# Interleaving xbc_proj with s5_mixer and rg_mixer, and re-staging four modulation vectors, in a two-block fp32 network

## The chip, the core and the metric

The kernel runs on one core of a Trainium2 chip: TensorE (PE; its weight loads are listed as PEld), VectorE (DVE), ScalarE (ACT), GpSimd (POOL) and SyncE (SP), which here only issues DMAs, each with its own in-order instruction stream, over one SBUF and one PSUM. The metric is device microseconds of one execution. A run's time is a little longer than the span of its trace, which goes from the first to the last instruction.

## What is computed

Two blocks in a row on 1024 tokens of width 1024, in float32. The first is a retention and gated-linear-attention mixer with an MLP, modulated by six vectors from a conditioning vector c. The second is a mixer of three parts (SSD, S5, RG-LRU), then cross attention, then an MLP. The lines that matter here:

```python
mod = jax.nn.silu(c) @ w_ada[l] + b_ada[l]
shift1, scale1, gate1, shift2, scale2, gate2 = jnp.split(mod, 6, axis=-1)
u = _layer_norm(x) * (1.0 + scale1[:, None, :]) + shift1[:, None, :]
...
proj = jnp.einsum('bld,dk->blk', h, w_in[l].astype(f32))
z, xbc, dt_raw, u_s5, x_rg, g_rg = jnp.split(proj, split_idx, axis=-1)
xbc = jax.nn.silu(causal_dwconv(xbc, conv_w.astype(jnp.float32), conv_b.astype(jnp.float32)))
y_s5 = s5_mixer(u_s5, ...)      # diagonal complex scan, gelu, gated linear unit
y_rg = rglru_mixer(x_rg, g_rg, ...)   # conv, two gates, real scan, times gelu(gate)
y = jnp.concatenate([y_ssd, y_s5, y_rg], axis=-1)
```

## The kernel before

Every large product is made of three passes over a high and a low half of its operands (mm3, lines 114 to 116). A weight page is loaded into a staging page of tag S, cast on ACT (L82) and its remainder made on DVE (L83); wcols does this for 256 columns, two staging pages and four pages of tag W. feat_out makes one 128 x 512 result from 24 matmuls into a PSUM bank of tag mm, of which there are two. SBUF is handed out in pages by tag, and the counts set how far work can run ahead: X 8, H 8, W 8, S 6, bc 3.

The order on each engine is not written by hand. The Tile framework takes the program's order as priority and plans every engine's order ahead of time, with its own estimates of durations: an instruction whose inputs and pages are there goes ahead of an earlier one that waits. On the chip each engine then keeps that order, whether or not the estimates were right. A generator's yield is a place where build can put another generator's instructions in between, so it moves priorities only.

Two places matter.

**The later modulation vectors.** scale1 and shift1 are made first (mod_first). The four others, of the order scale2, shift2, gate1, gate2, come from mods: mod_acc adds eight scaled row blocks of w_ada (512 KB each, loaded at L243, added on DVE at L245 and L247) into an accumulator page. mod_feat then takes it through 16 listed matmuls with a column of ones (L259), mod_row through L275, followed by an add and a store. Accumulator and row blocks are all pages of tag bc. mods and then s5_setup are the side generator early(), woven into gla_proj with 0.6 side steps for each of its 26 steps. gla_block, which is woven into the following ret_proj, takes its work pages E and qt from X.

**The input projections of the second mixer.** build calls dt_proj, s5_mixer, xbc_proj and rg_mixer one after the other. s5_mixer holds eight pages of X until its second matrix stage (L1625, L1628) and its gelu. xbc_proj makes eight pages of 128 channels (j = 0 to 7, weights c = j // 2) with two feat_outs each, evicted by ACT to two pages raw and o (L1193, L1194), convolved on DVE (L1176), passed through Tanh (L1197) and a product (L1198) and stored (L1199); raw and o are X pages. rg_mixer makes two feat_outs for each of two halves (L1316, L1317), gates (L1329 to L1334), a chain of Ln, Exp and Sqrt (L1338 to L1343) and a scan (L1345), then two gelu gates (L1351 to L1354) whose weights are Wg. ssd_setup, the loads of the output weights (wout_load, eight staging pages, L659) and the SSD blocks woven with block2_out come behind.

Of the kernel before, what the change touches and what calls it, by code (L numbers as in the profile page):

```python
# [14 lines left out]
S = 1024  # L15
# [9 lines left out]
class Net:  # L25
# [211 lines left out]
    def mod_acc(self, j):  # L237

        nc = self.nc
        acc = self.page("bc")  # L240
        for k in range(8):
            w = self.page("bc")
            nc.sync.dma_start(out=w, in_=self.I["w_ada"][k * 128:(k + 1) * 128, j * 1024:(j + 1) * 1024])  # L243
            if k == 0:
                nc.vector.tensor_scalar(out=acc, in0=w, scalar1=self.silu_c[:, 0:1], scalar2=None, op0=ALU.mult)  # L245
            else:
                nc.vector.scalar_tensor_tensor(out=acc, in0=w, scalar=self.silu_c[:, k:k + 1], in1=acc, op0=ALU.mult,  # L247
                                               op1=ALU.add)
            if k % 4 == 3:
                yield  # L250
        return acc

    def mod_feat(self, j, name, plus=0.0):

        nc = self.nc
        acc = yield from self.mod_acc(j)
        ps = self.ps("tr")
        for k in range(8):
            nc.tensor.matmul(out=ps[:, k:k + 1], lhsT=acc[:, k * 128:(k + 1) * 128], rhs=self.ones[:, 0:1],  # L259
                             start=True, stop=True)  # L260
        m = self.cp.tile([128, 8], F32, name=name)
        nc.vector.scalar_tensor_tensor(out=m, in0=ps[:, 0:8], scalar=plus, in1=self.pvec("b_ada")[:, 8 * j:8 * j + 8],
                                       op0=ALU.add, op1=ALU.add)
        self.mod[name] = m

    def mod_row(self, j, name):

        nc = self.nc
        acc = yield from self.mod_acc(j)
        g = self.small([128, 1024], tag="bc", bufs=self.BUFS["bc"])  # L270
        nc.sync.dma_start(out=g[0:1, :], in_=self.I["b_ada"][0:1, j * 1024:(j + 1) * 1024])
        for h in range(2):
            ps = self.ps()
            sl = slice(512 * h, 512 * h + 512)
            nc.tensor.matmul(out=ps[0:1, :], lhsT=self.ones[:, 0:1], rhs=acc[:, sl], start=True, stop=True)  # L275
            nc.vector.tensor_tensor(out=g[0:1, sl], in0=ps[0:1, :], in1=g[0:1, sl], op=ALU.add)
        d = self.dram([1, 1024], name)
        nc.sync.dma_start(out=d, in_=g[0:1, :])
        self.mod[name] = d

    def mods(self):
        yield from self.mod_feat(4, "scale2", 1.0)
        yield from self.mod_feat(3, "shift2")
        yield from self.mod_row(2, "gate1")
        yield from self.mod_row(5, "gate2")

    def normalize4(self, ys):

# [773 lines left out]
class Mix2(Mix1):  # L1062
# [116 lines left out]
    def xbc_proj(self, T):  # L1179
# [5 lines left out]
        for c in range(4):  # L1185
            W = self.wcols(I["w_in_2"], 512 + 256 * c, 256)
            for m in range(2):
                j = 2 * c + m
                raw, o = self.page("X"), self.page("X")
                for h in range(2):  # L1190
                    sl = slice(512 * h, 512 * h + 512)
                    ps = self.feat_out(T, W, slice(128 * m, 128 * m + 128), h)
# [4 lines left out]
                nc.scalar.activation(out=raw, in_=o, func=ACTF.Tanh)  # L1197
                nc.vector.scalar_tensor_tensor(out=o, in0=raw, scalar=1.0, in1=o, op0=ALU.add, op1=ALU.mult)  # L1198
                nc.sync.dma_start(out=self.s_xd[:, j, :], in_=o)  # L1199

    def ssd_setup(self):
        self.s_St = self.half()
# [88 lines left out]
    def rg_mixer(self, T):  # L1291
        nc, I = self.nc, self.I
        w = I["w_in_2"]
# [17 lines left out]
        for m in range(2):  # L1311
            raw, xc = self.page("X"), self.page("X")
# [5 lines left out]
                                     bias=cb[:, m:m + 1])  # L1318
            self.conv(xc, raw, cw[:, 4 * m:4 * m + 4])
            xcs.append(xc)  # L1320
        Wg = self.wcols(w, 2056, 256)
        ms = []
        for m in range(2):
# [10 lines left out]
            nc.scalar.activation(out=t, in_=r, func=ACTF.Tanh, scale=sm[:, 2 + m:3 + m])  # L1334
            nc.vector.scalar_tensor_tensor(out=gx, in0=gx, scalar=1.0, in1=xc, op0=ALU.add, op1=ALU.mult)
            ms.append((xc, r, gx, t))
        for m, (xc, r, gx, t) in enumerate(ms):
            nc.scalar.activation(out=xc, in_=t, func=ACTF.Ln, bias=1.0)  # L1338
            nc.scalar.activation(out=xc, in_=xc, func=ACTF.Exp, scale=-1.0)
# [2 lines left out]
        for m, (xc, r, gx, t) in enumerate(ms):  # L1342
            nc.scalar.activation(out=t, in_=t, func=ACTF.Sqrt, scale=0.5)  # L1343
            nc.vector.tensor_tensor(out=gx, in0=gx, in1=t, op=ALU.mult)
            nc.vector.tensor_tensor_scan(out=t, data0=r, data1=gx, initial=0.0, op0=ALU.mult, op1=ALU.add)  # L1345
        for m, (xc, r, gx, t) in enumerate(ms):
            x, q = self.page("X"), self.page("X")
            for h in range(2):
# [199 lines left out]
    def s5_mixer(self, T):  # L1548
# [54 lines left out]
        a = [v3(x)[:, :, i0] for x in (Are, Aim)]  # L1603
        p = [v3(x)[:, :, i0] for x in (co, sn)]
        self.cmul(v3(H[0])[:, :, i1], v3(H[1])[:, :, i1], a, p, v3(t)[:, :, i1])
        M = [self.page("H") for _ in range(2)]
        for m in range(2):
            for s in range(8):
# [9 lines left out]
        for m in range(2):  # L1618
# [28 lines left out]
                nc.scalar.activation(out=q[:, sl], in_=ps, func=ACTF.Square)  # L1647
            self.gelu(x, q, x)
            Y.append(x)
        gw = self.half([128, 2, 256])  # L1650
        nc.sync.dma_start(out=gw, in_=I["s5_glu_w_2"].rearrange("(k p) e -> p k e", p=128))
        gb = self.small([128, 8], tag="s5t", bufs=20)
# [130 lines left out]
def build(tc, I, out):  # L1783
    from contextlib import ExitStack
    with ExitStack() as ctx:
# [22 lines left out]
            T = next(norm)  # L1808
        run(kv)
        def early():  # L1810
            yield from n.mods()
            yield from n.s5_setup()
        run(n.weave(n.gla_proj(T), early(), 0.6))
        n.gla_setup()
        run(n.weave(n.ret_proj(T), n.pipe(n.gla_block(i) for i in range(NB)), 0.3))
        n.ret_setup()
# [3 lines left out]
        T = run(n.block1_out())  # L1820
        T = n.block1_mlp(T)
        n.dt_proj(T)
        n.s5_mixer(T)
        n.xbc_proj(T)
        n.rg_mixer(T)
        n.ssd_setup()
        n.wout = n.wout_load(I["w_out_2"])
        out = n.block2_out()
# [90 lines left out]
```

## Time and profile before

| | us |
|---|---|
| median of 3 runs (2730.89 to 2739.81) | 2733.69 |
| the profiled execution, its own time | 2723.2 |
| its span | 2721.4 |
| PE busy | 2572.5 (95%) |
| DVE busy | 1908.2 (70%) |
| ACT busy | 1113.8 (41%) |
| POOL busy | 265.8 (10%) |
| mean granted PE clock, as a share of full speed | 0.964 |

The profiled execution is 10.5 us below the median, and 1.8 us of its time lie outside the span. PE's busy share counts overlapped matmuls; the time between two matmuls of a dense run is what a stretch of PE work takes. A granted clock of 1.00 is the level of 2.4 GHz, 0.50 that of 1.2 GHz, and what lies between is a stretch that had some of both.

### The profile page before, as it was taken

To read this page: it belongs to the slowest core of one execution; us is meant where nothing else is said; L and a number is where in the kernel's file an instruction comes from. 1 tells how busy PE (TensorE), PEld (TensorE's weight loads), DVE (VectorE), ACT (ScalarE), POOL (GpSimd) and SP (SyncE) were. 2 spreads that over 40 slices of the span, in tenths; PEclk is the share of its full clock that TensorE was granted. 3 is DMA by queue.
4 is the path that set the end of the run, shared out by engine and by line. 5 is a ranking of instruction groups with operands and counts; after the bars stand their busy time and mean duration, and the time that the engine had idled before them with its cause. 6 is when DMAs were issued, how large, how long until landed. Compare 5 with 4: busy or idle time off the path is not lost.

```text
span 2721.4 us, 32892 instructions
## 1 busy us (share of the span) xinstructions
PE 2572.5 (95%) x12086; PEld 2085.6 (77%) x12086; DVE 1908.2 (70%) x3237; ACT 1113.8 (41%) x1669; POOL 265.8 (10%) x238
## 2 busy tenths in 40 slices
PE   7898999889999999999999997999997999999997
PEld 7576777677888888888876765778876888888885
DVE  5847765788897777555954558785566877767759
ACT  3522233224654444433642462452236444444332
POOL 4112135540000000000000004200000000000000
PEclk8899999999999999999997998999998999999998
DMA  9674423454266669857641313371101756699774
GB/s 332 210 232 142 147 98 102 142 150 147 78 224 217 214 234 324 287 177 240 202 153 47 110 62 105 111 242 40 54 21 73 246 195 224 230 325 333 271 234 145
DMA packets 255130, 484.36 MB, mean 178 GB/s; under 512 B 21604, under 2 KB 110964, under 8 KB 254968
## 3 DMA queue, kind: packets, MB, share of 16 engines
q1 hardware_dynamic: 247768, 470.59, 51.3%
q10 hardware_dynamic: 7200, 11.67, 1.2%
q8 instruction: 95, 1.56, 0.2%
q14 instruction: 67, 0.55, 0.1%
HBM read 338.80 MB, written 143.38 MB: 177 GB/s over the span
## 4 chain that ended last, share of the span: by engine, by line
PE 76%; DVE 10%; DMA 4%; ACT 4%; issue 3%; POOL 2%; SPq 0%; ACTq 0%; DVEq 0%; POOLq 0%
PE ps L114 23%; PE ps L116 23%; PE ps L115 23%; ACT half L186 1%; PE ps L182 1%; DMA H<-r_qk 1%; DVE half L543 1%; POOL X L522 1%; DMA H<-g_qkb 1%; DMA bc<-in_w_ada 1%; DVE st L155 1%; PE ps L1628 1%; DVE W L83 1%; PE ps L535 1%; POOL W L83 0%
## 5 line engine op out<-in xcount | busy, mean ns | idle before, releaser
L114 PE MATMUL ps<-U,W 128*128 128x512 f32 (+1 forms) x1080 | 426.2, 395 | 11.4 <-ACT X L1352 5.9
L83 DVE TENSOR_TENSOR W<-S,W 128x1024 fp32r<-128x1024 f32 (+1 forms) x272 | 332.8, 1225 | 147.9 <-ACT W L82 145.9
L114 PE MATMUL ps<-W,H 128*128 128x512 f32 x1088 | 425.1, 391 | 3.6 <-DVE sm L167 3.0
L115 PE MATMUL ps<-U,W 128*128 128x512 f32 (+1 forms) x1080 | 424.1, 393 | 0.1
L115 PE MATMUL ps<-W,H 128*128 128x512 f32 x1088 | 424.0, 390 | 0.0
L116 PE MATMUL ps<-W,H 128*128 128x512 f32 x1088 | 423.9, 390 | 0.0
L116 PE MATMUL ps<-U,W 128*128 128x512 f32 (+1 forms) x1080 | 423.5, 392 | 0.0
L82 ACT CAST W<-S 128x1024 fp32r<-128x1024 f32 x288 | 299.2, 1043 | 282.0 <-PE ps L115 200.0
L83 DVE TENSOR_TENSOR H<-S,H 128x1024 fp32r<-128x1024 f32 x130 | 158.8, 1222 | 149.3 <-ACT H L82 138.5
L82 ACT CAST H<-S 128x1024 fp32r<-128x1024 f32 x130 | 136.5, 1050 | 288.6 <-PE ps L115 211.9
L114 PEld LDWEIGHTS ps<-U,W 128*128 128x128 f32 (+1 forms) x1080 | 201.1, 186 | 59.9 <-ACT X L1352 6.3
L114 PEld LDWEIGHTS ps<-W,H 128*128 128x128 f32 x1088 | 204.6, 188 | 47.7 <-DVE X L1014 3.7
L115 PEld LDWEIGHTS ps<-U,W 128*128 128x128 f32 (+1 forms) x1080 | 201.1, 186 | 47.0 <-DVE U L336 2.5
L116 PEld LDWEIGHTS ps<-W,H 128*128 128x128 f32 x1088 | 204.4, 188 | 42.2 <-DVE H L83 0.2
L115 PEld LDWEIGHTS ps<-W,H 128*128 128x128 f32 x1088 | 204.6, 188 | 41.9
L116 PEld LDWEIGHTS ps<-U,W 128*128 128x128 f32 (+1 forms) x1080 | 200.7, 186 | 45.0 <-issue 0.7
L114 PE MATMUL ps<-W,U 128*128 128x512 f32 x352 | 142.0, 403 | 0.0
L115 PE MATMUL ps<-W,U 128*128 128x512 f32 x352 | 140.6, 399 | 0.2 <-DVE W L83 0.2
L116 PE MATMUL ps<-W,U 128*128 128x512 f32 x352 | 140.4, 399 | 0.1
L767 ACT ACTIVATE ev<-ev 128x512 f32<-128x512 f32 x104 | 65.5, 630 | 138.8 <-DVE ev L865 117.3
L1239 POOL TENSOR_TENSOR half<-tri,s_adt 128x512 f32<-128x512 f32 x16 | 19.6, 1233 | 884.5 <-DVE half L1116 778.2
L768 ACT ACTIVATE X<-ev 128x512 f32<-128x512 f32 x128 | 81.1, 636 | 3.5
(527 smaller groups left out, 4606.5 us busy)
## 6 DMA issues: line engine op xcount, KB each, us to landing
S<-mlp_h SPq DMA_DIRECT2D x112, 512.0 KB, 4.8
S<-in_w_ff SPq DMA_DIRECT2D x96, 512.0 KB, 5.1
mlp_h<-X SPq DMA_DIRECT2D x96, 512.0 KB, 3.9
S<-in_mlp_w SPq DMA_DIRECT2D x96, 512.0 KB, 5.2
mlp_w<-S SPq DMA_DIRECT2D x96, 256.0 KB, 2.8
S<-mlp_w SPq DMA_DIRECT2D x48, 512.0 KB, 4.8
S<-in_w_in SPq DMA_DIRECT2D x46, 512.0 KB, 5.2
bc<-in_w_ada SPq DMA_DIRECT2D x32, 512.0 KB, 5.0
```

Of the source, the lines that this page charges most:

```text
L82: self.nc.scalar.copy(out=hi, in_=src)
L83: (lo_eng or self.nc.vector).tensor_tensor(out=lo, in0=src, in1=hi.bitcast(F32), op=ALU.subtract)
L114: mm(out=ps, lhsT=lh, rhs=rh, start=start and k == 0, stop=False)
L115: mm(out=ps, lhsT=lh, rhs=rl, start=False, stop=False)
L116: mm(out=ps, lhsT=ll, rhs=rh, start=False, stop=stop and k == n - 1)
L155: self.nc.vector.bn_stats(out=st[:, h, :], in_=y[:, h * 512:(h + 1) * 512])
L182: nc.tensor.transpose(ps[:, j * 128:(j + 1) * 128], y[:, k * 128:(k + 1) * 128], self.ident)
L186: nc.scalar.activation(out=full[:, j * 128:(j + 1) * 128], in_=ps[:, j * 128:(j + 1) * 128], func=ACTF.Identity, scale=scale[:, k:k + 1], ...
L522: nc.gpsimd.tensor_tensor(out=E[:, l, :].rearrange("p (g c) -> p g c", c=2 * w), in0=bv, in1=bv[:, :, w - 1:w].broadcast_to([128, 64 // w, ...
L535: nc.tensor.matmul(out=ps[:, r, u, :], lhsT=k[rs] if l < 0 else E[rs, l, :], rhs=q[rs] if l < 0 else qt[rs, l, :], start=True, stop=True)
L767: nc.scalar.activation(out=r, in_=x, func=ACTF.Relu)
L768: nc.scalar.activation(out=out, in_=r, func=ACTF.Square)
```

## The change

mod_acc takes its row blocks from X pages, and mod_row its row page too; the accumulators stay in bc. mods first makes two accumulators and then sends each through PE only after the next one has been made, with two empty steps ahead of the last. early() begins with three empty steps, and the weave takes 0.75 side steps for each step of gla_proj. In the second mixer, xbc_proj becomes a generator with a yield behind each j, its raw pages come from S and its o pages from bc. s5_mixer gets two yields (behind the scan's rotation; ahead of the gated linear unit) and rg_mixer three (behind the convolution, the gates and the scan). At the first yield of s5_mixer three steps of xbc_proj are put in, at the second one, at the first of rg_mixer one and at the second three.

```diff
--- before.py
+++ after.py
@@ -239,7 +239,7 @@
         nc = self.nc
         acc = self.page("bc")
         for k in range(8):
-            w = self.page("bc")
+            w = self.page("X")
             nc.sync.dma_start(out=w, in_=self.I["w_ada"][k * 128:(k + 1) * 128, j * 1024:(j + 1) * 1024])
             if k == 0:
                 nc.vector.tensor_scalar(out=acc, in0=w, scalar1=self.silu_c[:, 0:1], scalar2=None, op0=ALU.mult)
@@ -250,10 +250,9 @@
                 yield
         return acc
 
-    def mod_feat(self, j, name, plus=0.0):
-
-        nc = self.nc
-        acc = yield from self.mod_acc(j)
+    def mod_feat(self, acc, j, name, plus=0.0):
+
+        nc = self.nc
         ps = self.ps("tr")
         for k in range(8):
             nc.tensor.matmul(out=ps[:, k:k + 1], lhsT=acc[:, k * 128:(k + 1) * 128], rhs=self.ones[:, 0:1],
@@ -263,11 +262,10 @@
                                        op0=ALU.add, op1=ALU.add)
         self.mod[name] = m
 
-    def mod_row(self, j, name):
-
-        nc = self.nc
-        acc = yield from self.mod_acc(j)
-        g = self.small([128, 1024], tag="bc", bufs=self.BUFS["bc"])
+    def mod_row(self, acc, j, name):
+
+        nc = self.nc
+        g = self.page("X")
         nc.sync.dma_start(out=g[0:1, :], in_=self.I["b_ada"][0:1, j * 1024:(j + 1) * 1024])
         for h in range(2):
             ps = self.ps()
@@ -279,10 +277,17 @@
         self.mod[name] = d
 
     def mods(self):
-        yield from self.mod_feat(4, "scale2", 1.0)
-        yield from self.mod_feat(3, "shift2")
-        yield from self.mod_row(2, "gate1")
-        yield from self.mod_row(5, "gate2")
+
+        a = yield from self.mod_acc(4)
+        b = yield from self.mod_acc(3)
+        self.mod_feat(a, 4, "scale2", 1.0)
+        a = yield from self.mod_acc(2)
+        self.mod_feat(b, 3, "shift2")
+        b = yield from self.mod_acc(5)
+        self.mod_row(a, 2, "gate1")
+        yield
+        yield
+        self.mod_row(b, 5, "gate2")
 
     def normalize4(self, ys):
 
@@ -1186,7 +1191,7 @@
             W = self.wcols(I["w_in_2"], 512 + 256 * c, 256)
             for m in range(2):
                 j = 2 * c + m
-                raw, o = self.page("X"), self.page("X")
+                raw, o = self.page("S"), self.page("bc")
                 for h in range(2):
                     sl = slice(512 * h, 512 * h + 512)
                     ps = self.feat_out(T, W, slice(128 * m, 128 * m + 128), h)
@@ -1197,6 +1202,7 @@
                 nc.scalar.activation(out=raw, in_=o, func=ACTF.Tanh)
                 nc.vector.scalar_tensor_tensor(out=o, in0=raw, scalar=1.0, in1=o, op0=ALU.add, op1=ALU.mult)
                 nc.sync.dma_start(out=self.s_xd[:, j, :], in_=o)
+                yield
 
     def ssd_setup(self):
         self.s_St = self.half()
@@ -1318,6 +1324,7 @@
                                      bias=cb[:, m:m + 1])
             self.conv(xc, raw, cw[:, 4 * m:4 * m + 4])
             xcs.append(xc)
+        yield
         Wg = self.wcols(w, 2056, 256)
         ms = []
         for m in range(2):
@@ -1334,6 +1341,7 @@
             nc.scalar.activation(out=t, in_=r, func=ACTF.Tanh, scale=sm[:, 2 + m:3 + m])
             nc.vector.scalar_tensor_tensor(out=gx, in0=gx, scalar=1.0, in1=xc, op0=ALU.add, op1=ALU.mult)
             ms.append((xc, r, gx, t))
+        yield
         for m, (xc, r, gx, t) in enumerate(ms):
             nc.scalar.activation(out=xc, in_=t, func=ACTF.Ln, bias=1.0)
             nc.scalar.activation(out=xc, in_=xc, func=ACTF.Exp, scale=-1.0)
@@ -1343,6 +1351,7 @@
             nc.scalar.activation(out=t, in_=t, func=ACTF.Sqrt, scale=0.5)
             nc.vector.tensor_tensor(out=gx, in0=gx, in1=t, op=ALU.mult)
             nc.vector.tensor_tensor_scan(out=t, data0=r, data1=gx, initial=0.0, op0=ALU.mult, op1=ALU.add)
+        yield
         for m, (xc, r, gx, t) in enumerate(ms):
             x, q = self.page("X"), self.page("X")
             for h in range(2):
@@ -1603,6 +1612,7 @@
         a = [v3(x)[:, :, i0] for x in (Are, Aim)]
         p = [v3(x)[:, :, i0] for x in (co, sn)]
         self.cmul(v3(H[0])[:, :, i1], v3(H[1])[:, :, i1], a, p, v3(t)[:, :, i1])
+        yield
         M = [self.page("H") for _ in range(2)]
         for m in range(2):
             for s in range(8):
@@ -1647,6 +1657,7 @@
                 nc.scalar.activation(out=q[:, sl], in_=ps, func=ACTF.Square)
             self.gelu(x, q, x)
             Y.append(x)
+        yield
         gw = self.half([128, 2, 256])
         nc.sync.dma_start(out=gw, in_=I["s5_glu_w_2"].rearrange("(k p) e -> p k e", p=128))
         gb = self.small([128, 8], tag="s5t", bufs=20)
@@ -1808,9 +1819,11 @@
             T = next(norm)
         run(kv)
         def early():
+            for _ in range(3):
+                yield
             yield from n.mods()
             yield from n.s5_setup()
-        run(n.weave(n.gla_proj(T), early(), 0.6))
+        run(n.weave(n.gla_proj(T), early(), 0.75))
         n.gla_setup()
         run(n.weave(n.ret_proj(T), n.pipe(n.gla_block(i) for i in range(NB)), 0.3))
         n.ret_setup()
@@ -1820,9 +1833,13 @@
         T = run(n.block1_out())
         T = n.block1_mlp(T)
         n.dt_proj(T)
-        n.s5_mixer(T)
-        n.xbc_proj(T)
-        n.rg_mixer(T)
+        xbc = n.xbc_proj(T)
+        for g, side in ((n.s5_mixer(T), (3, 1)), (n.rg_mixer(T), (1, 3))):
+            for _ in g:
+                for _ in range(side[0] if side else 0):
+                    next(xbc, None)
+                side = side[1:]
+        run(xbc)
         n.ssd_setup()
         n.wout = n.wout_load(I["w_out_2"])
         out = n.block2_out()
```

## Rows read from the trace of the kernel before

**Rows 1.** Page, part 2: 40 equal slices of the span, in tenths.
```profile
PE   7898999889999999999999997999997999999997
PEclk8899999999999999999997998999998999999998
```

**Rows 2.** Waits of PE, 100 to 310 us: in total, times, longest.
```profile
PE ps L275 <- DVE bc L247: 13.9, 2, 9.8
```

**Rows 3.** Windows, 180 to 240: length, PE, PEld, DVE, ACT, POOL busy, clock, DMA.
```profile
190.00:200.00 10.00, 10.00 (x35) 6.57 (x34) 4.69 (x7) 6.17 (x9) 7.59 (x16) 0.84 0.76 232
...
220.00:230.00 10.00, 4.38 (x7) 1.03 (x7) 4.59 (x6) 0.00 (x0) 0.00 (x0) 0.52 0.24 73
```

**Rows 4.** Waits of SP's queue, 60 to 310 us.
```profile
SPq L243 <- DVE bc L247: 39.9, 22, 5.7
SPq L243 <- DMA bc<-in_w_ada: 30.9, 16, 5.0
```

**Rows 5.** Page, part 6: DMA issues, KB each, median us to landing.
```profile
S<-in_w_in SPq DMA_DIRECT2D x46, 512.0 KB, 5.2
bc<-in_w_ada SPq DMA_DIRECT2D x32, 512.0 KB, 5.0
```

**Rows 6.** Timeline of DVE, 75 to 125 us: start, length, line, idle before.
```profile
102.08 1.28 DVE L247 SCALAR_TENSOR_TENSOR bc<-bc,silu_c,bc 128x1024 f32<-128x1024 f32 x1
```

**Rows 7.** Timeline of POOL: the gla blocks' first work, 191 to 320 us.
```profile
191.17 5.54 POOL L522 TENSOR_TENSOR X<-H 128x128 f32<-128x128 f32 x14 [99.88 <-DMA H<-g_qkb]
...
315.27 2.56 POOL L522 TENSOR_TENSOR X<-H 128x128 f32<-128x128 f32 x7 [95.77 <-PE ps L535]
```

**Rows 8.** Timeline of PE, 390 to 430 us: a gla block's wait.
```profile
398.87 0.80 PE L535 MATMUL ps<-H 64*128 64x128 f32 x4 [3.77 <-DVE half L543]
```

**Rows 9.** Timeline of PE, 1450 to 1500 us, without the projections' matmuls.
```profile
1455.16 1.22 PE L1628 MATMUL ps<-H,X 64*128 64x128 f32 x4 [5.44 <-DVE X L1362]
1457.66 0.79 PE L1628 MATMUL ps<-H,X 64*128 64x128 f32 x2 [1.28 <-DVE X L1365]
...
1485.05 1.22 PE L1628 MATMUL ps<-H,X 64*128 64x128 f32 x4
```

**Rows 10.** Windows of the second mixer, columns as in rows 3.
```profile
1458.00:1491.00 33.00, 33.00 (x109) 24.75 (x109) 5.63 (x7) 5.55 (x10) 0.00 (x0) 0.51 0.00 0
1491.00:1602.00 111.00, 111.00 (x469) 87.43 (x468) 65.17 (x54) 54.19 (x71) 1.04 (x1) 1.00 0.27 96
1602.00:1637.00 35.00, 29.08 (x119) 21.48 (x118) 21.36 (x20) 31.24 (x37) 1.37 (x1) 0.95 0.15 46
1637.00:1690.00 53.00, 38.07 (x163) 26.80 (x162) 47.66 (x70) 15.22 (x29) 31.85 (x21) 0.77 0.37 111
```

**Rows 11.** Timeline of ACT: evictions of xbc, casts of weights, 1428 to 1575 us.
```profile
1431.09 1.05 ACT L82 CAST W<-S 128x1024 fp32r<-128x1024 f32 x1 [1.67 <-PE ps L115]
...
1491.10 0.62 ACT L1193 COPY X<-ps 128x512 f32<-128x512 f32 x1
...
1515.39 0.59 ACT L1193 COPY X<-ps 128x512 f32<-128x512 f32 x1 [3.45 <-PE ps L116]
...
1520.83 0.59 ACT L1193 COPY X<-ps 128x512 f32<-128x512 f32 x1 [3.12 <-PE ps L116]
```

**Rows 12.** Timeline of DVE: the last use of bc, and a weight's remainder.
```profile
1380.07 1.23 DVE L1039 TENSOR_TENSOR X<-X,bc 128x1024 f32<-128x1024 f32 x1
...
1510.80 1.23 DVE L83 TENSOR_TENSOR W<-S,W 128x1024 fp32r<-128x1024 f32 x1 [0.59 <-ACT W L82]
```

**Rows 13.** Waits of PE, 1400 to 1660 us.
```profile
PE ps L114 <- ACT X L1352: 5.9, 1, 5.9
```

**Rows 14.** Timeline of ACT: table loads, first and last of seven, 1599 to 1626.
```profile
1598.99 1.28 ACT L1330 ACT_TABLE_LOAD   x1
...
1625.58 1.28 ACT L1244 ACT_TABLE_LOAD   x1
```

**Rows 15.** Waits of SP's queue, 1400 to 1660 us.
```profile
SPq L1199 <- DVE X L1198: 51.7, 7, 9.7
```

## Prediction

> **What bounds the kernel now.** The slices come first [rows 1]: PE is busy nearly everywhere; its busy share dips in the slice of 204 to 272 us, its clock, furthest of all, in that of 1429 to 1497, and both in that of 1633 to 1701. So the end is set by PE's own work plus the places where PE stands or runs at 1.2 GHz, and the change can only pay there. I then asked for PE's waits and the windows around these places.
>
> In the first place PE stands 13.9 us in two waits of the gate rows' products (L275) for the DVE sums of w_ada [rows 2]. Behind each wait the clock drops: 0.84 over ten fully busy microseconds, and 0.52 over 4.38 us of work [rows 3]. The reason lies one engine further on. With three bc pages, one of them the accumulator, two row blocks can be under way; SP waits 39.9 us in 22 waits for a page to be added up before it may issue the next load, and 30.9 us more on loads themselves [rows 4], while one load takes 5.0 us to land [rows 5]. The planned order put L275 where it thought the sum would be done.
>
> In the second place PE waits 5.44 and 1.28 us for the DVE chain of S5's scan, and then does the S5 matrices, which are small, at half speed until about 1485 [rows 9]: 33.00 us busy at a clock of 0.51 [rows 10]. There was work to fill this. ACT's first eviction of xbc comes only at 1491.10 although a weight page was cast at 1431.09 [rows 11]: xbc's raw and o pages are X, and S5 holds all eight X until its second stage. Two PSUM banks fill, and PE has nothing left. Later PE waits 5.9 us for a gelu eviction of rg (L1352), which stood on ACT behind the chain of Ln, Exp and Sqrt [rows 13], and from 1602 to 1637 PE is busy 29.08 us at 0.95 [rows 10].
>
> **The change, part by part.** *Modulation.* The row blocks move to X, eight pages against two, so the loads are no longer paced by one addition each; and each product is put one vector, eight loads, behind its sum. At 5.0 us for each load, even were they one after the other, that is 40 us of slack, more than the longest wait of 9.8 us [rows 2, 5]. I count both waits as gone: 13.9 us. The clock with them: 10.00 x 0.16 = 1.6 and 4.38 x 0.48 = 2.1, together 3.7 us [rows 3]. What is late next is PE's own dense projection work, which is what we want. Three steps of delay also keep the w_ada additions out of the first norm, where DVE was full; one addition of 1.28 us stood on that chain [rows 6]: 1.3 us. The 32 loads move behind the first loads of w_in on SP's queue; those are no longer behind them, and I count nothing for that.
>
> The price: X is what the gla blocks need for E and qt. In the trace the first ones use the pause to do their POOL part from 191.17 us, and after that none begins until 315.27 [rows 7]. With X full of row blocks they may come later and fall among the dense projections, where a block costs PE a wait such as the 3.77 us of L535 [rows 8]. Two blocks bound it at 7.5 us, and at nothing below, since the pause that they filled goes too. I take one, 3.8 us, as DVE is free again once the sums are done. s5_setup is listed four steps of gla_proj later but its input page no longer waits for three bc pages' worth of loads; no price.
> Sum: 13.9 + 3.7 + 1.3 - 3.8 = 15.1 us.
>
> *xbc in S5 and rg.* A feat_out costs PE 5.44 us, the distance of two evictions (1515.39 to 1520.83) [rows 11]. Three steps of xbc are six of these, 32.6 us, and they now stand ahead of S5's second stage. Two of them ran before the hole already, the other four are 21.8 us, against the 6.7 us that DVE was late: the waits of 5.44 and 1.28 us go, and the matrices come after dense work, so at full clock. That is 33.00 x 0.49 = 16.2 us [rows 9, 10]. The fourth step covers S5's gelu. In rg, the steps j = 5 to 7, again 32.6 us of PE work, stand between the gates and the Wg products, so that ACT can do its table functions below them and the 5.9 us wait goes, with 29.08 x 0.05 = 1.5 us of clock [rows 10, 13]. Together 5.44 + 1.28 + 5.9 + 16.2 + 1.5 = 30.3 us.
> DVE has the same work in a shorter stretch: it was busy 5.63, 65.17 and 21.36 us in the 179 us from 1458 to 1637 [rows 10], 92.2 in 149 after, 62%: covered. ACT, 91.0 of the same, likewise. The o pages are free: bc is used last at 1380.07 [rows 12].
>
> The price is in S. Before, all six staging pages ran ahead with weights; now two of them are raw pages that are held through the convolution and Tanh. If the next pair's weights can be asked for only when the second raw page before them has begun, they need 5.2 us to land, 1.05 us of ACT and 1.23 of DVE, 7.5 us, against the 5.44 us of the feat_out that is left: 2.1 us of PE wait [rows 5, 11, 12]. Four times weights are wanted so (c = 1, 2, 3 and rg's Wx); behind c = 0 S5's matrices cover it, so 3 x 2.1 = 6.2 us. Bounds: nothing, where other products fill in, and the rival below. I take 6.2.
> Sum: 30.3 - 6.2 = 24.1 us.
>
> Behind it the start of the SSD blocks (1637 to 1690, PE busy 38.07 of 53 at 0.77, DVE 47.66) [rows 10] is bound by DVE and POOL. It follows the end of rg and only moves forward; I count neither gain nor loss.
>
> A rule of the Trainium skill speaks against this part. The trace shows seven table loads of 1.28 us between 1599 and 1626 [rows 14], in rg alone; in the new order the Tanh passes of xbc stand among rg's Sigmoid, Ln, Exp and Sqrt. The Trainium skill, page "ScalarE: Activation LUTs", sections "What ACT_TABLE_LOAD costs" and "Table sets: the hidden batching unit", says that functions are to be grouped by set, and puts a switch at about 2.66 us with the engine's drain; the trace agrees on the load, and no row here shows the drain. By the page four passes with a switch in and out would cost ACT 8 x 2.66 = 21.3 us, called an estimate. By the row it is 8 x 1.28 = 10.2 us of ACT time, which evictions with two banks of 5.44 us each can stand; I take nothing for it in the sum.
>
> **The whole.** 15.1 + 24.1 = 39.2 us. The profiled execution's own time is 2723.2 (its span 2721.4 and 1.8 around it): 2684.0. The runs' median was 10.5 us above it, so 2694.5; I say **2694**.
>
> **The rivals.**
> *Only one of the two pays.* The order is planned anew everywhere and by estimates that were wrong at both places; a product may again be planned too early, or X may run dry through gla. For: L275 was misplaced by 9.8 us once. Against: both remedies are many times the lateness. Only the weave: 2733.7 - 24.1 = 2709.6. Only the modulation: 2733.7 - 15.1 = 2718.6. Within it lies the table rival: the 10.2 us of table loads come to stand before rg's evictions, and the 5.9 and 1.5 us do not go: 2694 + 7.4 + 2.8 = 2704, inside the forecast's range.
> *The start of SSD shrinks too.* rg's pages come free below xbc's products, so the SSD blocks could start beside dense work. PE's loss from 1637 to 1690 is 14.9 us idle and 38.07 x 0.23 = 8.8 of clock; half of it and no price in S or X: 2733.7 - 49.2 - 11.8 = 2673.
> *Slower: weights starve in S.* SP's queue is in order. The stores of xbc wait on it for DVE 51.7 us in seven waits, 9.7 at most [rows 15]. That was harmless because the weights had been loaded far ahead. If a weight load now stands behind such a store, PE pays 7.5 + 9.7 = 17.2 us at each of the four changes of weights, 69 us, and falls to 1.2 GHz behind each. Against the 30.3 us of the weave that is 38 us lost, with the modulation's 15.1 a time of about 2757. It decides where a pair's load is issued later than 7.5 us before the last matmul of the pair in use; raw pages held one at a time, not two, would keep it away, and S5 and rg can fill some of it.
> *No change.* Both parts are planned around and the stalls come back elsewhere: 2734.
>
> **How the numbers follow.** Forecast (2680 to 2708): 0.60. One part alone (2708 to 2722): 0.18. SSD's start too (about 2673): 0.08. No change: 0.06. Slower: 0.08. The range 2674 to 2722 leaves out the last two and part of the third, under 0.2; its ends are the sum without prices and half the SSD loss, and the weave failing. 0.3% is 8.2 us, about what a measurement of this kernel can tell from no change: faster 0.86, within it 0.06, slower 0.08.
>
> **What would show it.** Right: no wait of PE for L247 behind L275 between 180 and 240 us, and a clock of 1.00 there; the w_ada loads closer together and done before 200; evictions of xbc some 40 us earlier than 1491; the S5 matrices at half their length; no 5.9 us wait for L1352. Wrong: PE waiting for casts (W, L82 or L83) at the changes of xbc's weights; SP standing at L1199 with a load of w_in next; a gla stretch, 310 to 490, longer than before; more table loads than seven in rg, with evictions late behind them.

## Result and the profile after

The changed kernel takes 2688.14 us (median of 4 runs, 2684.58 to 2695.17), the kernel before beside it 2732.29: a ratio of 0.9836, 95% interval 0.9809 to 0.9864, some 44 us. The two profiled executions lie closer together, 2721.4 and 2686.1 us of span, 35.3 us; executions of the kernel before differ by more than 20 us among themselves (last section). The one profiled (2723.2 us) was shorter than all four of these, but lies in the middle of the 27 that ran beside the experiments. In another set of runs the same pair of kernels gave 2723.09 and 2689.62 us, a ratio of 0.9887 (0.9859 to 0.9916), 33.5 us. So 44 us is at the upper end of what was seen, and the profiled pair stands for the rest. The accounts below are of the profiled pair.

Where the time went is seen first by marking the same store in both traces (last DMA issue for each tensor, from the views by tile):

| last store of | before | after | shift |
|---|---|---|---|
| gg (end of gla_proj) | 294.6 | 279.0 | -15.6 |
| r_qk (ret_proj) | 489.6 | 481.1 | -8.5 |
| r_od (last retention block) | 640.2 | 632.7 | -7.5 |
| s_z (dt_proj) | 1396.9 | 1389.6 | -7.3 |
| rg_od (rg_mixer) | 1653.0 | 1615.0 | -38.0 |
| s_od (last SSD block) | 1792.5 | 1757.2 | -35.3 |
| end of span | 2721.4 | 2686.1 | -35.3 |

So the modulation's part brought 7.5 us, and the weave 28.0, less 0.2 in between; behind the SSD blocks nothing moved. The 15.6 us at gg are not all gain: the change also moved work behind this store, as the account below shows. The page's slices of the kernel after, the busy share of PE and its clock in tenths, answer [rows 1]. Busy share: the dip near 204 to 272 us is filled, the one near 1633 to 1701 is weaker. Clock: the deepest dip, at 1429 to 1497, is gone; the one near 1650 stays, and a small one has come at 537 to 604 us:

```profile
PE   7899999889999999999999998999988999999997
PEclk8899999989999999999999998999998999999998
```

**Modulation.** The DMA issues of the page (KB each, median us to landing) answer [rows 5]: a row block now takes longer to land, but many are under way.

```profile
S<-in_w_in SPq DMA_DIRECT2D x46, 512.0 KB, 5.7
X<-in_w_ada SPq DMA_DIRECT2D x32, 512.0 KB, 6.7
```

They are issued from 82.6 to 153.5 us, against 70.4 to 220.6 before. The wait of 13.9 us [rows 2] has no counterpart. In its place PE stands at another point. These are PE's waits from 200 to 216 us, ACT's timeline there (start, length, line; in brackets the idle time before it and what ended it), and the windows (columns as in [rows 3]):

```profile
PE ps L273 <- ACT ev L438: 2.9, 1, 2.9
PE ps L114 <- DVE X L274: 0.8, 1, 0.8
PE ps L114 <- ACT ev L438: 0.3, 1, 0.3
```

```profile
200.91 0.59 ACT L438 COPY ev<-ps 128x512 f32<-128x512 f32 x1 [0.40 <-ACT ev L438]
...
201.89 1.28 ACT L1431 ACT_TABLE_LOAD   x1 [0.39 <-ACT ev L438]
209.35 0.21 ACT L1431 ACTIVATE s5t<-s5t 128x8 f32<-128x8 f32 x1 [6.18 <-DVE s5t L1430]
...
209.56 0.56 ACT L438 COPY ev<-ps 128x512 f32<-128x512 f32 x1
```

```profile
200.00:206.00 6.00, 5.67 (x26) 4.43 (x24) 5.46 (x19) 2.38 (x4) 2.29 (x2) 1.00 0.23 89
206.00:214.00 8.00, 4.25 (x9) 1.08 (x8) 6.91 (x50) 0.78 (x3) 0.00 (x0) 0.72 0.08 33
214.00:224.00 10.00, 10.00 (x33) 7.99 (x33) 10.00 (x94) 2.72 (x3) 2.64 (x7) 0.71 0.03 13
```

L438 is the eviction of gla_v's PSUM banks. Between two of them ACT has the Sin of s5_setup (L1431; its table load is listed under the same line), and it waits there 6.18 us for a chain of small DVE instructions. The next eviction stands behind it, both banks stay full, and PE can start neither the next projection nor the gate row (L273). It idles some 4 us, and its clock falls: 4.25 x 0.28 + 10.00 x 0.29 = 4.1 us more.

In the kernel before, the same Sin (L1422 there) stood between two evictions of gla_v too, but without a wait: DVE had done the chain from 229.84 to 236.06 us, while PE, just out of its old wait, made one product.

```profile
235.99 0.59 ACT L433 COPY ev<-ps 128x512 f32<-128x512 f32 x1 [19.30 <-PE ps L116]
236.59 1.28 ACT L1422 ACT_TABLE_LOAD   x1
...
237.89 0.21 ACT L1422 ACTIVATE s5t<-s5t 128x8 f32<-128x8 f32 x1
```

PE's waits of the whole gla stretch, 150 to 560 us, first before, then after:

```profile
PE ps L535 <- DVE half L543: 18.7, 12, 5.5
```

```profile
PE ps L540 <- DVE half L548: 22.3, 13, 5.5
```

**The second mixer.** ACT evicts the first bank of xbc at 1436.50, not at 1491.10 [rows 11]:

```profile
1436.50 0.59 ACT L1198 COPY S<-ps 128x512 f32<-128x512 f32 x1 [7.38 <-PE ps L116]
```

The windows of the stretch, shifted with the work, answer [rows 10]. The 33 us at a clock of 0.51 have gone; the clock is 1.00 throughout until the SSD blocks start, in the last line:

```profile
1436.00:1491.00 55.00, 53.53 (x266) 42.57 (x265) 35.86 (x31) 17.72 (x27) 0.00 (x0) 1.00 0.30 92
1491.00:1540.00 49.00, 49.00 (x196) 36.28 (x194) 28.87 (x25) 27.01 (x35) 1.41 (x1) 1.00 0.16 57
1540.00:1575.00 35.00, 33.52 (x133) 24.24 (x132) 18.45 (x16) 34.73 (x40) 0.00 (x0) 1.00 0.32 106
1575.00:1602.00 27.00, 26.66 (x119) 21.43 (x118) 21.83 (x19) 13.73 (x19) 0.00 (x0) 1.00 0.61 196
1602.00:1655.00 53.00, 39.19 (x184) 27.95 (x183) 47.99 (x73) 16.65 (x32) 30.44 (x21) 0.87 0.38 112
```

PE's groups of S5's matrices (busy us, mean ns | idle), before, then after: 460 and 467 ns for one have become 299 and 318, and the 6.7 us of waits are gone. Counted from start to start, a group of four L1628 and two L1625 took 1.87 us before (1459.10 to 1460.97) and takes 1.06 after (1474.26 to 1475.32): 57%, not quite the half that a clock of 0.51 suggests.

```profile
L1628 PE MATMUL ps<-H,X 64*128 64x128 f32 x64 | 19.1, 460 | 6.7 <-DVE X L1362 5.4 <-DVE X L1365 1.3
L1625 PE MATMUL ps<-H,X 128*128 128x128 f32 x32 | 11.6, 467 | 0.0
```

```profile
L1638 PE MATMUL ps<-H,X 64*128 64x128 f32 x64 | 11.1, 299 | 0.0
L1635 PE MATMUL ps<-H,X 128*128 128x128 f32 x32 | 7.5, 318 | 0.0
```

PE's waits from 1380 to 1640 us; of the projections only the changes of weights (W) are left, 2.9 us, and of the 5.9 us for rg's gelu [rows 13] 0.2:

```profile
PE ps L1249 <- POOL half L1245: 5.7, 2, 4.8
PE ps L114 <- ACT W L82: 2.1, 2, 1.1
...
PE ps L116 <- DVE W L83: 0.8, 2, 0.5
...
PE ps L114 <- ACT X L1361: 0.2, 1, 0.2
```

An account of PE's losses for each part: idle time is the length less the busy time of windows of 10 us that begin anew at each marker, the clock's loss is busy time x (1 - clock). The clock's loss depends on where the windows are cut (without the cut at gg the first stretch has 28.1 before and 27.3 after), so a difference of 1 us in it says nothing.

| stretch | before: length, idle, clock | after: length, idle, clock |
|---|---|---|
| 60 us to the last store of gg | 234.6, 22.2, 13.2 | 219.0, 11.9, 13.6 |
| last gg to last r_od | 345.6, 40.9, 13.3 | 353.7, 44.5, 13.1 |
| both | 580.2, 63.1, 26.5 | 572.7, 56.4, 26.7 |
| last s_z to 1637 us before, 1602 after (SSD start) | 240.1, 12.6, 17.9 | 212.4, 3.3, 0.0 |
| last s_z to last s_od | 395.6, 32.7, 28.1 | 367.6, 22.2, 6.9 |

The modulation's gain is idle time alone, 6.7 us. At gg it has 9.9 us of idle time and clock; the other 5.7 of the 15.6 are work that PE now does later (960 recorded matmuls ahead of this store against 1009). Behind gg 3.6 us of idle time come back, 2.9 of them in longer waits for the gla blocks' halves before the first store of r_qk (5.3 us against 2.4). From that store to the last of r_od both traces take the same time, 279.4 us before and 280.0 after.

The weave's gain is made ahead of the SSD start, where the account closes: 9.3 us of idle time and 17.9 of clock, together 27.2 of the 27.7 us by which the stretch is shorter. Over the whole stretch to s_od it does not close (10.5 + 21.2 = 31.7 against 28.0): in the 53 us of the SSD start PE now does more, 184 recorded matmuls against 163, in the same length.

### The profile page after: what moved, and what is told of

It reads as the page before. It is cut to its first block, busy times and chain, and to the rows that moved or that the text cites. A ratio compares the mean times of both kernels' runs of the same rounds, so it can differ in the third digit from the quotient of the medians.

```text
span 2686.1 us, 32858 instructions
## 1 busy us (share of the span) xinstructions
PE 2554.4 (95%) x12086; PEld 2073.2 (77%) x12086; DVE 1905.0 (71%) x3237; ACT 1114.9 (42%) x1671; POOL 262.0 (10%) x238
## 3 DMA queue, kind: packets, MB, share of 16 engines
q1 hardware_dynamic: 247768, 470.59, 51.7%
## 4 chain that ended last, share of the span: by engine, by line
PE 75%; DVE 10%; ACT 4%; DMA 4%; issue 4%; POOL 3%; SPq 0%; POOLq 0%; DVEq 0%; ACTq 0%
PE ps L114 23%; PE ps L115 23%; PE ps L116 23%; ACT half L186 1%; DMA H<-r_qk 1%; PE ps L182 1%; DVE half L548 1%; DVE W L83 1%; DMA S<-in_xa_wk 1%; POOL X L527 1%; PE ps L540 1%; DVE st L155 1%; DMA H<-g_qkb 1%; POOL W L83 0%; DVE U L341 0%
## 5 line engine op out<-in xcount | busy, mean ns | idle before, releaser
L773 ACT ACTIVATE X<-ev 128x512 f32<-128x512 f32 x128 | 81.1, 636 | 3.5
```

The costliest lines, as they stand in the source:

```text
L773: nc.scalar.activation(out=out, in_=r, func=ACTF.Square)
```

## Experiments

**The parts by themselves.** Each takes one part of the change into the kernel before.

```diff
 # weave_only: mods as before; the rest as changed
-            w = self.page("X")
+            w = self.page("bc")
...
-            for _ in range(3):
-                yield
...
-        run(n.weave(n.gla_proj(T), early(), 0.75))
+        run(n.weave(n.gla_proj(T), early(), 0.6))
 # mods_only: the modulation as changed; s5_mixer, xbc_proj, rg_mixer as before
```

> The kernel before with only the second mixer's part of the change (raw in S, o in bc, the yields, three and one steps of xbc in S5, one and three in rg); the modulation vectors are as before. Theory, read from the two traces: this part carries most of the gain, 28 us (between the last store of s_z and the last store of s5_od the changed kernel is 28.0 us shorter), so about 28 us faster than the kernel before, ratio 0.990. By the prediction's steps it would be 24.1 us, ratio 0.991. Rival: the gains of the two parts hang on each other (less work ahead of S5 or another order), then less than 20 us.

> The kernel before with only the modulation's part of the change (row blocks in X, products one vector later, three empty steps, 0.75). Theory, read from the two traces: about 7.3 us faster, ratio 0.9973, with a new stall of PE near 207 to 214 us, where ACT's evictions of gla_v stand behind the Sin of s5_setup. By the prediction's steps 15.1 us, ratio 0.9945. Rival: nothing (ratio 1.000), if the shift of the markers in the trace after came from elsewhere.

weave_only: 2696.68 us, ratio 0.9895 (0.9857 to 0.9932). mods_only: 2713.93 us, ratio 0.9968 (0.9945 to 0.9991), beside 2725.1 for the kernel before. The profiled spans are 2694.0 and 2713.4, that is 27.4 and 8.0 us below 2721.4, and 27.4 + 8.0 = 35.4 is the 35.3 of the whole change: in the profiled executions the parts add up and do not hang on each other. By the medians they are 28.4 and 11.2 us, and the interval of mods_only just reaches the 15.1 us of the prediction's steps (0.9945); that its part is near 8 us rests on the traces. In both traces the markers go with it: weave_only has its last s_z store at 1395.2 and its last s_od store at 1765.2, mods_only at 1389.6 and 1784.1.

**The pages of xbc without its place.**

```diff
-        xbc = n.xbc_proj(T)
-        for g, side in ((n.s5_mixer(T), (3, 1)), (n.rg_mixer(T), (1, 3))):
...
-        run(xbc)
+        run(n.s5_mixer(T))
+        run(n.xbc_proj(T))
+        run(n.rg_mixer(T))
```

> The changed kernel with the second mixer called in its old order: all of s5_mixer, then all of xbc_proj, then all of rg_mixer; raw stays in S and o in bc. Theory that pages held xbc back: the planner runs what is ready, so with S and bc free it fills S5's hole itself; the two waits for the scan go and part of S5's matrices run at full clock, 15 to 22 us of the 28 stay, and rg keeps its wait for gelu: 6 to 13 us slower than the changed kernel, 22 to 29 us faster than the kernel before. Theory that the written order does it: 3 to 8 us of the 28 stay, some 20 to 25 us slower than the changed kernel.

2695.41 us, ratio 0.9884 (0.9856 to 0.9912); its span of 2694.4 is 8.3 us above the changed kernel's. From the last s_z store to the last s_od store it takes 374.3 us, 21.3 less than before, 6.7 more than the changed kernel. So the pages do three quarters of the 28.0, and the written order adds the rest once they are there; the written order without the pages was not run. With S and bc to go to, xbc fills the hole in S5 although it is listed behind all of S5, as the windows of pages_only show against 33.00 us at 0.51 in [rows 10]:

```profile
1430.00:1458.00 28.00, 28.00 (x179) 23.40 (x175) 25.35 (x22) 6.53 (x10) 4.33 (x3) 1.00 0.21 66
1458.00:1491.00 33.00, 31.41 (x148) 21.83 (x149) 16.90 (x18) 15.78 (x21) 1.04 (x1) 1.00 0.19 64
```

What the written order adds is in rg, where the old wait stands again in PE's waits of pages_only:

```profile
PE ps L114 <- ACT X L1361: 5.9, 1, 5.9
PE ps L1257 <- DVE half L1267: 4.1, 2, 2.5
```

**The new stall.** The first part of s5_setup, with its Sin, goes ahead of the modulation vectors.

```diff
+        s5 = n.s5_setup()
         def early():
             for _ in range(3):
                 yield
+            next(s5)
+            yield
             yield from n.mods()
-            yield from n.s5_setup()
+            yield from s5
```

> The changed kernel with the first part of s5_setup (up to its first yield: the exponentials, both Sin, the powers) one place earlier, ahead of the modulation vectors; the rest of s5_setup stays behind them. Theory that the modulation's missing gain went to the new stall: ACT no longer waits 6.18 us for the small DVE chain between two evictions of gla_v, PE's waits of 2.92 and 0.83 us go, and its clock stays (8.00 and 10.00 us at 0.72 and 0.71 cost some 4.1 us): 7.8 us faster than the changed kernel, about 2680. Rival: the chain is no shorter and stands in the evictions of the first norm, where DVE is full; the stall is only moved, and the time is 2688 or above.

> The kernel of sin_first once more, as the base of the three beside it. If its gain over the changed kernel is real: 2678 to 2687 us, and again no wait of PE between 205 and 220 us. If the clock loss of the stall only moves: a mean granted clock of 0.973 to 0.975, as in the changed kernel, and a dip of the clock somewhere between 280 and 480 us that the changed kernel does not have.

2684.02 us, ratio 0.9839 (0.9807 to 0.9870), and in the second set 2682.16, ratio 0.9841 (0.9822 to 0.9859). The changed kernel has 2688.14 and 2689.62, 4 to 7.5 us more, less than the 7.8 expected or just short of it. The two were not run side by side, and by the ratios to the kernel before, 0.9839 and 0.9841 against 0.9836 and 0.9887, the gain is not clear of noise; the traces have to show it. The place is clean in both traces; here sin_first:

```profile
200.00:206.00 6.00, 6.00 (x33) 5.10 (x33) 1.75 (x1) 1.75 (x2) 6.00 (x9) 1.00 0.03 11
206.00:214.00 8.00, 7.92 (x35) 6.24 (x34) 2.30 (x3) 2.19 (x5) 3.39 (x2) 1.00 0.18 68
214.00:224.00 10.00, 10.00 (x46) 6.54 (x45) 8.84 (x9) 4.30 (x5) 0.00 (x0) 1.00 0.73 227
```

The last store of gg comes 7.4 us earlier than in the changed kernel. But in the first profiled execution only 3.4 are left at the last store of r_od: idle time from 60 us on is 53.2 against 56.4, and the clock's loss 26.3 against 26.7, since the clock now drops between 280 and 310 (granted 0.89 there, 1.00 in the changed kernel). In the profiled execution of the second set the r_od store is 8.1 us earlier and the clock's loss from 60 to 629 us 20.0. So the idle time is won in both traces, and the clock in one of them. That the stall cost the changed kernel about 8 us is shown where it stands: up to the last store of gg idle time and clock's loss together are 25.5 us in the changed kernel and 17.1 in sin_first; how much of it reaches the end depends on the clock behind it.

**Pages or place in the modulation.** One run keeps X and puts each product right behind its sum; the other keeps the place and puts the row blocks in bc.

```diff
 # x_pages_old_order
-        a = yield from self.mod_acc(4)
-        b = yield from self.mod_acc(3)
-        self.mod_feat(a, 4, "scale2", 1.0)
+        a = yield from self.mod_acc(4)
+        self.mod_feat(a, 4, "scale2", 1.0)
+        a = yield from self.mod_acc(3)
...
 # bc_pages_new_order
-            w = self.page("X")
+            w = self.page("bc")
```

> The changed kernel as it is, on the chip of the three runs beside it, so that they are compared with it there: ratio 0.982 to 0.986 against the kernel before, 2684 to 2692 us, PE's waits for W in the woven stretch 2.9 us in all, its waits for the gla blocks' halves (L540) some 22 us between 100 and 490 us.

> The changed kernel with each product of a modulation vector right behind its own sum again (scale2, shift2, gate1, gate2 one after the other); the row blocks still come from X, the three empty steps and 0.75 stay. Theory that the pages did it: the loads run far ahead of the sums, no wait for L247 of over 2 us is left, and the time is within 3 us of the changed kernel. Theory that the place did it: the product is planned where the sum is thought to be done, and waits of 5 to 10 us for L247 come back, 5 to 14 us slower than the changed kernel.

> The changed kernel with the row blocks of the modulation vectors in bc again; the products stay one vector behind. With two accumulators held, one of three bc pages is left for row blocks: one load of 5.0 us and one sum of 1.3 us at a time, 32 x 6.3 = 202 us, against 71 us of loads in the changed kernel. Theory that the pages did it: the sums end near 285 us, PE waits for them 8 us or more in all, and the time is 5 to 20 us above the changed kernel. Theory that the place alone does it: no wait for L247 over 2 us, and within 3 us of the changed kernel.

On one chip: the changed kernel 2689.62 us, ratio 0.9887 (0.9859 to 0.9916); with X and the old place 2691.30, 0.9894 (0.9859 to 0.9929); with bc and the new place 2698.20, 0.9916 (0.9883 to 0.9949). The changed kernel's time is as expected, its ratio is not (0.982 to 0.986), as the kernel before took 2723.09 here. PE's waits from 190 to 250 us, with X and the old place, then with bc and the new one:

```profile
PE ps L114 <- DVE X L274: 8.6, 2, 5.1
```

```profile
PE ps L273 <- DVE bc L247: 7.1, 2, 4.6
PE ps L114 <- DVE X L274: 0.7, 1, 0.7
```

With X no wait for a sum (L247) is left even where the product stands right behind it, so the pages took away what the prediction was about. A wait of another kind comes: the add of the gate row (L274), which frees the bank, stands on DVE among the small instructions of s5_setup. By their times this run and the changed kernel can't be told apart. With bc the loads take from 81.1 to 232.6 us, some of the old wait is back, 7.1 us, half of the 13.9 that the kernel before had with bc and the old place. The median is 8.6 us above the changed kernel's, but the intervals overlap, and the execution in the trace was the shortest of its four (2691.73 us, against 2691.55 for the changed kernel's traced one). I had expected the sums to end near 285; they end at 239, since a load is issued each 4.9 us and not each 6.3. Why is not shown.

**The slower rival.** xbc's o pages also go to S.

```diff
-                raw, o = self.page("S"), self.page("bc")
+                raw, o = self.page("S"), self.page("S")
```

> The changed kernel with xbc's o pages in S as well as its raw pages, so that they are held until the store has read them and up to four of the six staging pages are gone. It tests the prediction's slower rival. By the rival's price a change of weights costs PE 7.5 + 9.7 = 17.2 us, four of them 69 us, and the time is above the kernel before (near 2755). Theory that S5 and rg fill it: PE's waits for W (L82, L83) in the woven stretch go from 2.9 us to 8 to 20 us, and the time is 5 to 20 us above the changed kernel, still below the kernel before.

2688.53 us, ratio 0.9884 (0.9854 to 0.9914): no different from the changed kernel beside it (2689.62). The waits for W are 2.6 and 0.8 us against 2.1 and 0.8:

```profile
PE ps L114 <- ACT W L82: 2.6, 2, 1.6
...
PE ps L116 <- DVE W L83: 0.8, 2, 0.5
```

So neither theory's number holds: with both pages of xbc in it, S still makes PE wait no longer. What makes the changed kernel's 2.9 us is read on ACT, not in S. At the first change of weights the cast of the next weights stands behind a Tanh that waits for the convolution, though the Tanh is not urgent.

```profile
1447.86 0.79 ACT L1199 ACTIVATE bc<-ps,hw 128x512 f32<-128x512 f32 x1
1451.74 1.06 ACT L1202 ACTIVATE S<-bc 128x1024 f32<-128x1024 f32 x1 [3.09 <-DVE bc L1181]
1452.71 1.02 ACT L82 CAST W<-S 128x1024 fp32r<-128x1024 f32 x1
```

The load had been issued at 1426.68, 26 us earlier. At the other change, near 1555, the two casts stand in ACT's fullest stretch, 34.73 of 35 us in the windows above, among rg's functions and their table loads of 1.28 us (one at 1551.42, one at 1555.88 between the casts); the waits there are 1.4 of the 2.9 us. That this order causes the wait is argued from the trace; it was not tried.

**The gla blocks.** Three runs on top of sin_first move the blocks against ret_proj.

```diff
-        run(n.weave(n.ret_proj(T), n.pipe(n.gla_block(i) for i in range(NB)), 0.3))
+        run(n.weave(n.ret_proj(T), delay(n.pipe(n.gla_block(i) for i in range(NB)), 2), 0.3))   # gla_two_steps_later
+        run(n.weave(n.ret_proj(T), n.pipe(n.gla_block(i) for i in range(NB)), 0.25))            # gla_rate_0_25
+        run(n.weave(n.ret_proj(T), n.pipe(n.gla_block(i) for i in range(NB)), 0.4))             # gla_rate_0_4
```

> sin_first with the gla blocks two side steps later in the weave with ret_proj. Theory that the gla blocks cost what they cost wherever they stand (each is a back and forth of PE and DVE, planned with the same estimate): PE's waits for their halves stay at 20 to 24 us in all, and the time is within 5 us of sin_first. Rival, that they give back the modulation's gain because they begin too early: the waits fall to the 18.7 us of the kernel before or below, 4 us or more faster than sin_first.

> sin_first with 0.25 instead of 0.3 side steps of the gla blocks for each step of ret_proj, so more dense work stands between them. Theory of a fixed cost: waits of 20 to 24 us, within 5 us of sin_first, or slower where the last blocks are left without dense work beside them. Rival: fewer waits, 4 us or more faster.

> sin_first with 0.4 side steps of the gla blocks for each step of ret_proj, so the blocks stand closer together. Theory of a fixed cost: waits of 20 to 24 us, within 5 us of sin_first. Rival: less dense work between the blocks, waits of 28 us or more, 5 us or more slower than sin_first.

The medians are 2691.04, 2677.70 and 2689.09 beside 2682.16 for sin_first; the ratios 0.9874 (0.9856 to 0.9893), 0.9824 (0.9804 to 0.9844) and 0.9867 (0.9850 to 0.9885). PE's waits for the blocks' halves, in the order sin_first_again, two steps later, 0.25, 0.4:

```profile
PE ps L540 <- DVE half L548: 22.3, 12, 5.3
```

```profile
PE ps L540 <- DVE half L548: 13.6, 10, 5.3
```

```profile
PE ps L540 <- DVE half L548: 12.9, 10, 3.2
```

```profile
PE ps L540 <- DVE half L548: 31.8, 9, 5.5
```

The theory of a fixed cost falls: the waits go from 12.9 to 31.8 us with the rate. But they are not the time either. Two steps later has 8.7 us less of them than sin_first and is 8.9 us slower; its last gla store comes at 534.9 instead of 522.4, and its idle time from 60 to 629 us is 56.3 instead of 52.7, so what it saves in these waits it loses elsewhere in the stretch; the clock's loss there is also higher, 26.4 us against 20.0. The rate of 0.4 is only 2.2 us behind sin_first at the last r_od store and loses 5.3 more from there to the last s_z store. At 0.25 the idle time is 48.2 and the median the lowest of all, 4.5 us below sin_first, but the intervals overlap and the two profiled spans are the same (2679.3 and 2679.4): that it beats 0.3 is not shown. It is 10 to 12 us below the changed kernel's two medians, though not run beside it, and the version to try first.

## Why the prediction was right, point by point

It said 2694 and 2688.1 was measured; its sum of 39.2 us for the profiled execution was 35.3. The two terms missed in opposite directions: the modulation by 15.1 - 7.5 = 7.6 us too much, the weave by 28.0 - 24.1 = 3.9 too little. That these partly cancel is luck; both mechanisms, waits and half clock taken away by pages and order, are what the traces show.

- *The waits for the sums, 13.9 us.* Right, and for the reason given: the loads run ahead in X. The pages alone do it (x_pages_old_order), while the new place with bc pages only halves the wait, to 7.1 us (bc_pages_new_order).
- *The clock there, 3.7 us.* Not won in the profiled execution: the loss to the last gg store is 13.2 before and 13.6 after, as the new stall drops the clock in its place. Without that stall it is 9.1 (sin_first), so the term was right in size.
- *s5_setup later, no price.* This is the step that failed. I looked at when its input page arrives and not at where its instructions come to stand on ACT and DVE. They stand between evictions of gla_v, as they did before, but ACT's pause of 19.30 us, at whose end their chain ran, is gone, and they cost some 4.0 us of idle time and 4.1 of clock: 8.1 us, about the modulation's shortfall of 7.6. With the Sin moved away, idle time and clock up to gg fall by 18.3 us (from 22.2 + 13.2 to 8.0 + 9.1 in sin_first), near the 18.9 that the three terms for this place add up to.
- *The gla blocks, 3.8 us.* Measured 22.3 - 18.7 = 3.6, and it belongs to the modulation (21.6 in mods_only, 18.8 in weave_only), but not by the way argued: X did not run dry. In both traces POOL does its part of two blocks in the pause (last at 215.71 us after, 208.81 before) and goes on with the third, at 304.37 after and 315.27 before [rows 7]. With the row blocks in X and the old place the waits are 19.4 us (x_pages_old_order). What lengthens them is not shown.
- *One sum on the first norm's chain, 1.3 us.* Not shown. One L247 is still there, at 99.39, and the first store of g_qkb comes at 129.1 after 130.6, but at 128.1 in weave_only, which leaves the modulation alone.
- *The waits for S5's scan and rg's gelu, 12.6 us, and the clock, 17.7.* Right: 6.7 us are gone and 5.9 have become 0.2. The clock's loss ahead of the SSD start falls by 17.9 us.
- *The SSD start, nothing.* Right in time. Over 53 us idle time goes from 14.9 to 13.8 and the clock's loss from 8.8 to 39.19 x 0.13 = 5.1, 4.8 us less in all. But this is no shorter stretch: it begins and ends 35 us earlier, as the last s_od store does, and PE puts 21 more recorded matmuls into it. The rival of an SSD start in half would have won 11.8.
- *The price in S, 6.2 us.* 2.9, and not in S: the mechanism was wrong, and with it the slower rival's. These 3.3 us are most of the weave's 3.9. The stores of xbc make SP wait even longer, 110.5 us in eight waits against 51.7 in seven [rows 15], and loads of weights do stand right behind such stores, at 1474.02 and 1544.12; but ACT casts these only at 1491.90 and 1554.82, when they had landed by the page's 5.7 us.
- *Table loads, taken as nothing.* Right in effect, or nearly. From 1536 to 1573 us there are nine where there were seven [rows 14], not eight more, and no eviction among them makes PE wait (the 0.2 us above stand behind 1580). The last load of either count is for the SSD blocks (L1244, L1250), not for rg. How much of the 1.4 us of waits for casts near 1555 is due to table loads is not shown. The Trainium skill, page "ScalarE: Activation LUTs", section "What ACT_TABLE_LOAD costs", counts a drain beside the load. The trace does not show it here: the last load begins at 1572.03, 0.02 us behind the end of the activation before it, and lasts 1.28 us, and its activation begins 0.01 us behind it.

```profile
1571.23 0.78 ACT L1199 ACTIVATE bc<-ps,hw 128x512 f32<-128x512 f32 x1
1572.03 1.28 ACT L1250 ACT_TABLE_LOAD   x1
1573.32 0.60 ACT L1250 ACTIVATE half<-ps 128x512 f32<-128x512 f32 x1
```

- *The offset of 10.5 us from the profiled execution to the median.* Carried over to the changed kernel, and it was not there: the profiled execution of the kernel after took 2687.83 us, its median 2688.14. It came from the set of runs: the 27 others of the kernel before have a median of about 2725 us, 2 above the profiled one. With 2684.0 alone the forecast would have been 4 us low rather than 6 high.

## What to carry to other kernels

When work is moved out of a stall, look on each in-order engine at what will stand between the evictions there: one small activation that waits for a chain of DVE instructions held two PSUM banks and cost some 8 us, near half of the 17.6 of the stall of which it took the place. Where a planner runs what is ready, pages rather than the written order decide what can fill a hole; here they gave 21 of 28 us. The shift of a marker is a gain only where the same work lies ahead of it: 5.7 of the 15.6 us at gg were work put off. And the rate of the next weave is worth trying again afterwards: 0.4 and a later start of the gla blocks were 7 to 9 us slower than 0.3.

## What the runs showed of the hardware

The spread between executions goes mostly with the clock. The kernel before, whose S5 matrices run at half clock, lay between 2709 and 2733 us in the 27 runs beside the experiments, and its time goes with the mean granted clock: 2711.43 us at 0.970, 2716.27 at 0.968, 2724.21 at 0.962, 2732.63 at 0.960, though not in every run (2717.27 at 0.963). mods_only, which keeps that hole, lay between 2708 and 2725; the eight runs of the changed kernel between 2685 and 2695 at 0.971 to 0.975. So a change that takes away a hole may also narrow the spread; the kernels with and without it were not run equally often, and the four runs of the kernel before in the result span only 9 us, so this is not shown. The difference of two medians, 44 us in the result, need not be that of two traces, 35.
